# Moving two small tiles and shortening a constants vector in a two-layer encoder kernel

## The chip, the cores and the metric

One core of a Trainium2 chip runs the whole program in one launch. The metric is device time in microseconds (us). [...]

## The reference

Two layers over 256 tokens of width 1024, all in float32. Each layer normalises, projects once into three groups of heads and adds the output projection; then follows a channel mixer, dense in layer 0 and a mixture of eight experts (two for each token) in layer 1.

```
for l in range(2):
    h = rmsnorm(x, norm_mix[l]); proj = h @ w_in
    x = x + concat([rwkv7(proj), diff_attention(proj), pool(proj)]) @ w_out[l]
    h = rmsnorm(x, norm_ffn[l])
    if l == 0: x = x + (silu(h @ w_gate) * (h @ w_up)) @ w_down
    else:      x = x + sum_e combine[:, e] * swiglu(h, expert e)   # top 2 of 8 by h @ router
return rmsnorm(x, norm_out)
```

## The kernel before, in words

**Matmuls.** A product of two float32 matrices is split into high and low halves of type float32r (`mm3`, line 266 and after): high by high, high by low, low by high, three matmuls that add up in one PSUM bank. `wload` (line 186) brings a weight tile of 512 KB into a raw tile by a DMA on SP's queue (line 197), ScalarE casts it to the high half (line 200), VectorE or GpSimd subtracts to get the low half (line 208). In the dense layer's gate and up products the weight halves are the stationary operand and the layer's input `fT` (256 columns) is the moving one; in its down product, and in the experts, the weight halves move (512 columns). `plain` (line 179, DMA on line 183) loads weights that are used as float32, without the split, for the experts with few tokens.

**Order of the work.** The sequence of TensorE is written out by hand. SP's queue takes the weight loads in program order, and one load that waits holds up all behind it. VectorE, ScalarE and GpSimd (POOL) also run their own instructions in order.

**Memory.** A partition of SBUF is filled from below by pools in the order in which they are opened: constants (`const`, with `x`, `ident`, `vecs`, `dvecs`, ...), the ring of weight tiles (`ring`: 4 raw, 3 high, 3 low tiles of 4096 bytes), the mixers' pool (`mixc`), and above it the pool of the present stage (`mix0`, `ffn0`, `mix1`). Every tile takes a multiple of 32 bytes. In the kernel before, the constants end at byte 26880 and the ring at 67840, both multiples of 256, and `mixc` begins there. In `mixc` stand, in order of first use, `hT_h` and `hT_l` (8192 bytes each, the normalised input's halves, at 67840 and 76032), `Z`, `vfirst`, the tile with tag `G` (at 92416; it holds `u`, then the dense layer's input `fT`, then `xT`), `rst`, `consts` (109824 to 114752), then the small tiles `i4` (114752, 128 bytes), `rksel`, `dtmp` (64 bytes), `nlam`, `sin`, `cos` and a filler `mcpad`. The stage pools begin at 115200, also a multiple of 256. `x` and `ident` stand at 128 mod 256.

After layer 1's mixer the pool `mixc` is closed, and the pool of the experts takes its place from 67840 on: first `tri` (512 bytes), a few small tiles, the one-hot matrices, and then 4096-byte tiles for weights, `r0`, `r1`, ... A new tile waits for the last readers of the older tiles whose bytes it covers (`reuse_waits="tile"`), and for no others. `LOADS` gives the order in which weight loads take the tiles: `r17`, `r18`, `r19`, `r5`, two of the ring's own, `msilu`, and so on, 28 entries. `r18` covers bytes 114176 to 118272.

**The start of the experts.** `i4` is read for the last time by the matmuls that add up the router's logits at the end of `outproj` (line 225 by way of `mm`, tile `i`). The routing is then: `lg` on VectorE, the comparisons `cmp` (lines 1443 to 1446), `rank`, `sel`, a product with `tri` on TensorE, the one-hot `Pm`, the gather. On POOL stand in this order: the load of `router` (line 1004) and its product with the gains (line 1005), two low-half splits (line 208), `one` (line 1390), `tri` (line 1392), the low halves of `x` (line 1424), two more splits (line 208).

Of the kernel before, what the change touches and what calls it, by code (L numbers as in the profile page):

```python
# [7 lines left out]
F32 = mybir.dt.float32  # L8
# [97 lines left out]
class K:  # L106
# [172 lines left out]
    def setup_x(self, P):  # L279
        nc, A, cp, mc = self.nc, self.A, self.cp, self.mc  # L280
        x = self.x = cp.tile([128, 2, D], F32, name="x")
        self.ident = cp.tile([128, 128], F32, name="ident")
        nc.sync.dma_start(self.ident, A["consts"][:, C_ID:C_ID + 128])
        self.v = cp.tile([128, NROWS], F32, name="vecs")
        dv = self.dv = cp.tile([128, 64], F32, name="dvecs")
        nc.vector.memset(dv[:, 43:59], -0.5)
        nc.vector.memset(dv[:, 42:43], -math.log(2.0))
        xv = A["x"][0].rearrange("(a p) d -> p a d", p=128)

        rows = P.tile([NROWS, 128], F32, name="rows", tag="at", bufs=2)  # L290
        nc.sync.dma_start(rows, A["rows"])
        for a in range(2):
            nc.sync.dma_start(x[:, a], xv[:, a])
        pb = self.bank("pr")
        self.tr(pb[:, :NROWS], rows, self.ident[:NROWS, :NROWS])
        nc.vector.tensor_copy(self.v, pb[:, :NROWS])

    def setup(self, P):
        nc, A, cp, mc, v, dv = self.nc, self.A, self.cp, self.mc, self.v, self.dv

        self.Z = mc.tile([128, 3, 2, 2, 128], F32, name="Z")
        self.vfirst = mc.tile([128, 2, 256], F32, name="vfirst")
        mc.tile([128, 4096], F32, name="G0", tag="G")
        self.rst = mc.tile([128, 256], F32, name="rst")
        c = self.c = mc.tile([128, C_W], F32, name="consts")
        self.i4 = mc.tile([128, 32], F32, name="i4")
        self.rks, tmp = mc.tile([128, 4, 2], F32, name="rksel"), mc.tile([128, 16], F32, name="dtmp")
        self.nlam = mc.tile([128, 2], F32, name="nlam")
        self.sin, self.cos = (mc.tile([128, 2, 8], F32, name=n) for n in ("sin", "cos"))
        mc.tile([128, 16], F32, name="mcpad")  # L310
        nc.scalar.dma_start(c, A["consts"][:, :C_W])
        self.c2 = cp.tile([128, C_ALL - C_IOTA], F32, name="consts2")
        nc.scalar.dma_start(self.c2, A["consts"][:, C_IOTA:])

        sh = v[:, ROW_SHIFT:ROW_SHIFT + 32].rearrange("p (l i k) -> p l i k", l=2, i=2)
        self.tmp = tmp
        t2 = tmp.rearrange("p (l k) -> p l k", l=2)
        nc.vector.tensor_add(t2, sh[:, :, 0], sh[:, :, 1])
        nc.vector.tensor_scalar(dv[:, 0:16], tmp, -1.0, 1.0, op0=ALU.mult, op1=ALU.add)
        nc.vector.tensor_scalar(dv[:, 16:32], v[:, ROW_DEC:ROW_DEC + 16], 0.5, None, op0=ALU.mult)  # L320
        nc.vector.tensor_scalar(dv[:, 32:36], v[:, ROW_KA:ROW_KA + 4], -1.0, 2.0, op0=ALU.mult, op1=ALU.add)
        nc.vector.tensor_scalar(dv[:, 36:40], v[:, ROW_RK:ROW_RK + 4], 0.5, None, op0=ALU.mult)
        nc.vector.tensor_scalar(dv[:, 40:42], v[:, ROW_VB:ROW_VB + 2], 0.5, None, op0=ALU.mult)

        rks = self.rks
        for i in range(4):
            nc.vector.tensor_scalar(rks[:, i, :], c[:, C_BLK:C_BLK + 128:64], dv[:, 36 + i:37 + i], None, op0=ALU.mult)
        with self.later():
            nc.gpsimd.memset(self.Z, 0.0)
        nc.vector.memset(self.rst, 1.0)  # L330
        nc.vector.memset(self.rst.rearrange("p (c t) -> p c t", t=64)[:, :, 0:1], 0.0)
        nc.vector.tensor_reduce(self.i4, self.ident.rearrange("p (g t) -> p t g", t=32), axis=AX.X, op=ALU.add)
# [1521 lines left out]
    def build(self):  # L1854
        nc, tc, cp = self.nc, self.tc, self.cp
        mixers = ExitStack()
        mc = self.mc = mixers.enter_context(tc.tile_pool(name="mixc", bufs=1))
        for l in range(DEPTH):
            with tc.tile_pool(name=f"mix{l}", bufs=1, reuse_waits="tile") as P, self.psum(f"pm{l}", pq=2, at=2, pr=3, py=1):
                self.mixer(l, P)  # L1860
            if l == DEPTH - 1:
                mixers.close()
            if self.stop == f"mix{l}":
                mixers.close()
                return
            with tc.tile_pool(name=f"ffn{l}", bufs=1, reuse_waits="tile") as P:
                if l % 2 == 0:
                    with self.psum(f"pf{l}", pa=4, pr=4):
                        self.ffn(l, P)
                else:  # L1870
                    with self.psum(f"pf{l}", pg=4, py=2, px=2):
                        self.moe(l, P)
            if self.stop == f"ffn{l}":
                mixers.close()
                return
# [39 lines left out]
```

## Time and profile before

| what | us |
|---|---|
| median of 3 runs | 1556.11 (1555.88 to 1558.05) |
| the profiled execution, its own time | 1553.22 |
| its span, first to last instruction | 1551.4 |
| busy: TensorE, VectorE, ScalarE, GpSimd | 1463.6, 1003.6, 806.2, 178.4 |
| DMA traffic | 434.67 MB, mean 280 GB/s |

How to read it: the program goes through layer 0's mixer (to about 190 us), the dense layer (to 440), layer 1's mixer (to 628), and the experts (to the end). TensorE's busy share of 94% is an average over these; a stage may be held by the loads while TensorE looks busy, since a matmul's duration is longer than the distance to the next one's start. So the distance of starts is what tells TensorE's pace, and the windows' DMA share what the loads carry.

### The profile page before, as it was taken

The page shows a single profiled execution, that of the slowest core. Times are in us where ns is not written, and L with a number is a line of the kernel's source. Part 1 is how long each engine was busy: PE and PEld are TensorE (multiplying, and loading weights), DVE is VectorE, ACT ScalarE, POOL GpSimd, SP SyncE. Part 2 cuts the span into 40 slices and gives each one's busy share as a digit, 9 for nine tenths or more (in the row PEclk, how much of TensorE's full clock was granted, in tenths as well). Part 3 has the DMA queues.
Part 4 walks back from the last instruction along what each step waited for, and adds up shares of the span by engine and source line. Part 5 has one row for each costly group of instructions (what it writes and reads, how often), then busy time and mean ns, then how long its engine had stood idle before and what let it go on. Part 6 is the DMA issues. An engine that isn't in the chain of part 4 may idle for free.

```text
span 1551.4 us, 27151 instructions
## 1 busy us (share of the span) xinstructions
PE 1463.6 (94%) x10215; PEld 1111.4 (72%) x10215; DVE 1003.6 (65%) x1314; ACT 806.2 (52%) x1142; POOL 178.4 (11%) x161
## 2 busy tenths in 40 slices
PE   7799989999998999799999999999998999998996
PEld 6677889999986778688888743588634687435885
DVE  5865665556659746698899720699512898205896
ACT  4545454444445354587878510687302776205785
POOL 2532100000026423300001000001000010000001
PEclk9899999999998899899999999999999999999998
DMA  7322356666543230899999999999999999999991
GB/s 230 104 70 98 109 166 188 186 182 189 163 120 95 70 125 3 310 412 410 338 332 348 353 407 415 410 411 413 403 419 412 410 411 412 389 416 411 410 413 43
DMA packets 172457, 434.67 MB, mean 280 GB/s; under 512 B 14834, under 2 KB 18013, under 8 KB 172317
## 3 DMA queue, kind: packets, MB, share of 16 engines
q1 hardware_dynamic: 170924, 430.74, 74.4%
q8 instruction: 82, 1.34, 0.3%
q0 software_dynamic: 544, 1.12, 0.3%
q10 hardware_dynamic: 848, 0.99, 0.2%
q14 instruction: 59, 0.48, 0.1%
HBM read 431.75 MB, written 1.05 MB: 279 GB/s over the span
## 4 chain that ended last, share of the span: by engine, by line
PE 75%; DVE 9%; DMA 7%; ACT 3%; issue 3%; POOL 1%; ACTq 0%; SPq 0%; DVEq 0%; POOLq 0%
PE ps L225 72%; PE ps L229 3%; DMA r<-in_exp_up 2%; DMA raw<-in_exp_up 2%; DMA r<-in_exp_gate 2%; DVE wlo L208 2%; DVE wlox L208 1%; DMA posi<-in_positions 1%; ACT whi L200 1%; ACT whix L200 0%; DVE AR L655 0%; DMA x<-in_x 0%; DVE us L550 0%; DVE kd L659 0%; ACT Sf L761 0%
## 5 line engine op out<-in xcount | busy, mean ns | idle before, releaser
L208 DVE TENSOR_TENSOR wlo<-r,whi 128x1024 fp32r<-128x1024 f32 x192 | 234.6, 1248 | 42.3 <-ACT whi L200 41.1
L200 ACT CAST whi<-r 128x1024 fp32r<-128x1024 f32 x195 | 201.0, 1056 | 37.5 <-DMA r<-in_exp_gate 19.3
L208 DVE TENSOR_TENSOR wlox<-r,whix 128x1024 fp32r<-128x1024 f32 x120 | 147.1, 1246 | 65.3 <-ACT whix L200 64.2
L200 ACT CAST whi<-raw 128x1024 fp32r<-128x1024 f32 x119 | 124.7, 1052 | 97.4 <-PE ps L225 82.6
L208 DVE TENSOR_TENSOR wlo<-raw,whi 128x1024 fp32r<-128x1024 f32 x104 | 129.7, 1251 | 59.7 <-ACT whi L200 59.3
L200 ACT CAST whix<-r 128x1024 fp32r<-128x1024 f32 x120 | 124.5, 1056 | 36.9 <-DMA r<-in_exp_gate 25.1
L225 PE MATMUL ps<-whi,gf 128*128 128x512 f32 x400 | 137.2, 401 | 1.3 <-ACT whi L200 1.3
L225 PE MATMUL ps<-r,gs 128*64 128x512 f32 (+1 forms) x636 | 130.6, 541 | 2.6 <-DMA r<-in_exp_up 2.5
L225 PE MATMUL ps<-fT,whi 128*128 128x256 f32 x544 | 100.8, 287 | 4.7 <-DVE gu L1306 3.7
L1417 POOL TENSOR_TENSOR xp<-x,xp 128x512 fp32r<-128x512 f32 x12 | 24.3, 2026 | 631.6 <-ACT xp L1416 631.6
L225 PE MATMUL ps<-whix,gf 128*128 128x512 f32 x272 | 93.9, 400 | 2.5 <-ACT whix L200 2.5
L225 PEld LDWEIGHTS ps<-r,gs 128*64 128x64 f32 x636 | 42.8, 136 | 74.1 <-issue 58.3
L225 PEld LDWEIGHTS ps<-whi,gf 128*128 128x128 f32 x400 | 76.6, 191 | 21.9 <-ACT whi L200 2.9
L225 PEld LDWEIGHTS ps<-fT,whi 128*128 128x128 f32 x544 | 86.2, 194 | 6.0 <-issue 4.3
L1663 ACT COPY mah<-ps 128x512 f32<-128x512 f32 (+1 forms) x12 | 6.4, 532 | 143.9 <-PE ps L229 143.9
L225 PE MATMUL ps<-wlo,gf 128*128 128x512 f32 x200 | 79.6, 398 | 1.2 <-DVE wlo L208 1.1
L225 PE MATMUL ps<-fT,wlo 128*128 128x256 f32 x272 | 77.6, 285 | 0.0
L225 PE MATMUL ps<-whi,hT_h 128*128 128x512 f32 x160 | 69.6, 435 | 5.6 <-DVE up L1073 5.5
L208 DVE TENSOR_TENSOR wlox<-raw,whix 128x1024 fp32r<-128x1024 f32 x51 | 63.1, 1242 | 17.5 <-ACT whix L200 16.6
L225 PE MATMUL ps<-r,mah 128*64 128x512 f32 x276 | 64.8, 599 | 2.4 <-DMA r<-in_exp_down 2.0
L225 PE MATMUL ps<-whi,mah 128*128 128x512 f32 x170 | 66.5, 391 | 0.0
L225 PE MATMUL ps<-wlo,mah 128*128 128x512 f32 x170 | 66.4, 390 | 0.0
(468 smaller groups left out, 3400.3 us busy)
## 6 DMA issues: line engine op xcount, KB each, us to landing
r<-in_exp_down SPq DMA_DIRECT2D x178, 512.0 KB, 10.1
r<-in_exp_up SPq DMA_DIRECT2D x172, 512.0 KB, 10.0
r<-in_exp_gate SPq DMA_DIRECT2D x172, 512.0 KB, 10.0
raw<-in_exp_gate SPq DMA_DIRECT2D x43, 512.0 KB, 10.0
raw<-in_exp_up SPq DMA_DIRECT2D x43, 512.0 KB, 9.9
raw<-in_exp_down SPq DMA_DIRECT2D x37, 512.0 KB, 10.0
raw<-in_w_in_first SPq DMA_DIRECT2D x22, 512.0 KB, 4.3
raw<-in_w_in_rest SPq DMA_DIRECT2D x22, 512.0 KB, 3.6
```

The source lines that it names most:

```text
L200: w1 = nc.scalar.copy(hi[:, :a * b], raw[:, :a * b])
L208: w2 = (early or nc.vector).tensor_sub(lo[:, :a * b], raw[:, :a * b], hi[:, :a * b].bitcast(F32))
L225: self.nc.tensor.matmul(out, lhsT, rhs, start=start, stop=stop, skip_group_check=skip_group_check)
L229: self.nc.tensor.transpose(out, in_, ident)
L1417: nc.gpsimd.tensor_sub(xl, xs, xh.bitcast(F32))
L1663: nc.scalar.copy(at, b)
```

## The change

The constants vector `dvecs` becomes 56 columns instead of 64 (32 bytes shorter; its unused tail of -0.5 is shortened with it). `i4` and `dtmp` are allocated first in `mixc`, when that pool is opened, instead of in `setup`. No instruction but the one memset differs.

By the allocator's rules that makes these places: the ring, the stage pools, the experts' pool and the rest of `mixc`'s small tiles lie 32 bytes lower (weights at 224 mod 256); `mixc`'s large tiles, the dense layer's input among them, lie 160 bytes higher (160 mod 256).

```diff
-        dv = self.dv = cp.tile([128, 64], F32, name="dvecs")
-        nc.vector.memset(dv[:, 43:59], -0.5)
+        dv = self.dv = cp.tile([128, 56], F32, name="dvecs")
+        nc.vector.memset(dv[:, 43:56], -0.5)
...
-        self.i4 = mc.tile([128, 32], F32, name="i4")
-        self.rks, tmp = mc.tile([128, 4, 2], F32, name="rksel"), mc.tile([128, 16], F32, name="dtmp")
+        self.rks, tmp = mc.tile([128, 4, 2], F32, name="rksel"), self.dtmp
...
         mc = self.mc = mixers.enter_context(tc.tile_pool(name="mixc", bufs=1))
+
+        self.i4, self.dtmp = mc.tile([128, 32], F32, name="i4"), mc.tile([128, 16], F32, name="dtmp")
```

## Rows read from the trace of the kernel before

**Rows 1.** Windows: us, busy us of each engine (instructions), granted clock, DMA share, GB/s

```profile
590.00:628.00 38.00, 36.79 (x288) 30.09 (x287) 21.29 (x45) 16.75 (x30) 13.27 (x11) 1.00 0.02 2
645.00:753.00 108.00, 106.76 (x480) 88.33 (x481) 98.03 (x127) 83.17 (x90) 0.00 (x0) 0.98 1.04 411
753.00:892.00 139.00, 138.47 (x644) 111.92 (x644) 120.28 (x120) 101.35 (x127) 9.76 (x4) 1.00 0.93 335
892.00:1527.00 635.00, 618.67 (x2867) 385.16 (x2864) 360.13 (x358) 303.91 (x372) 14.56 (x8) 0.99 1.01 402
```

**Rows 2.** SP's queue, timeline 540 to 632: start us, duration us

```profile
562.24 0.71 SPq L197 DMA_DIRECT2D r<-in_exp_up  x1
628.14 0.37 SPq L197 DMA_DIRECT2D r<-in_exp_gate  x1
```

**Rows 3.** SP's waits, 560 to 640: us in total, times, longest

```profile
SPq L197 <- PE ps L225: 65.1, 1, 65.1
```

**Rows 4.** Tiles i4 (named i) and nlam: min/median/max ns, first and last start us

```profile
L225 PE MATMUL ps<-i,router x4: 256/256/277, 627.5 to 627.9; 128*128 128x8 f32 x4
L1208 DVE SCALAR_TENSOR_TENSOR lamr<-lamr,nlam,smx x8: 210/217/1320, 133.3 to 592.5; 128x2 f32<-128x2 f32 x8
```

**Rows 5.** SP's waits, 750 to 800

```profile
SPq L197 <- DVE wlo L208: 22.8, 14, 5.5
```

**Rows 6.** POOL, timeline 605 to 640: start us, duration us

```profile
608.21 1.01 POOL L1004 DMA_DIRECT2D router<-in_router  x1
611.46 0.67 POOL L1005 TENSOR_TENSOR router<-router,vecs 128x64 f32<-128x64 f32 x1 [2.24 <-DMA router<-in_router]
616.87 2.41 POOL L208 TENSOR_TENSOR wlo<-w4o,whi 128x1024 fp32r<-128x1024 f32 x1 [4.74 <-ACT whi L200]
...
624.36 0.62 POOL L1392 TENSOR_SCALAR tri<-consts,vecs 128x128 f32<-128x128 f32 x1
626.85 4.73 POOL L1424 TENSOR_TENSOR x<-x,x 128x1024 fp32r<-128x1024 f32 x2 [1.86 <-ACT x L1423]
```

**Rows 7.** Chain of waits in order of time: start us, length us

```profile
628.35 1.02 DVE cmp L1443
629.38 2.37 DVE cmp L1444
...
669.62 16.38 PE ps L225 x72
```

**Rows 8.** Page, part 6: loads, KB each, median us from issue to landing

```profile
r<-in_exp_down SPq DMA_DIRECT2D x178, 512.0 KB, 10.1
...
lnw<-in_lnx_w POOLq DMA_DIRECT2D x2, 128.0 KB, 6.1
```

**Rows 9.** TensorE, timeline 619.2 to 619.8

```profile
619.53 0.39 PE L225 MATMUL ps<-wlo,hT_h 128*128 128x512 f32 x1
```

**Rows 10.** TensorE, timeline 300 to 300.9; between the two rows lie eight matmuls

```profile
299.75 0.28 PE L225 MATMUL ps<-fT,wlo 128*128 128x256 f32 x1
...
300.83 0.28 PE L225 MATMUL ps<-fT,wlo 128*128 128x256 f32 x1
```

**Rows 11.** TensorE, timeline 653 to 655; between the two rows lie four matmuls

```profile
652.61 0.63 PE L225 MATMUL ps<-whi,gh 128*128 128x512 f32 x1
...
654.74 0.63 PE L225 MATMUL ps<-whi,gl 128*128 128x512 f32 x1
```

**Rows 12.** Window 194 to 440, instructions that read or write fT: PE, PEld, DVE, ACT

```profile
194.00:440.00 246.00, 165.47 (x1344) 163.93 (x1344) 3.19 (x12) 1.99 (x8) 0.99 0.57 172
```

**Rows 13.** TensorE by line, 194 to 440 and 645 to 892: count, busy us, mean ns

```profile
L229 PE MATMUL ps<-ident,x 128*128 128x128 f32 x10 | 1.4, 272 | 0.0
...
L229 PE MATMUL ps<-ident,msilu 128*128 128x128 f32 x52 | 7.8, 271 | 0.0
```

**Rows 14.** DMA queue 1 in 4 to 6.2 and 7 to 9: packets, MB, share of 16 engines

```profile
q1 hardware_dynamic: 295, 0.88, 102.0%
...
q1 hardware_dynamic: 230, 0.82, 101.2%
```

## The prediction

> **What bounds the kernel now.** I read the windows first, cut at the places where the DMA share changes, then SP's queue with its waits, then POOL's timeline and the chain of waits around the start of the experts, and last TensorE's starts. Three things are to be seen.
>
> Before the experts the loads stand still: from 590 to 628 us the DMA share is 0.02 [rows 1]. SP issued one expert load at 562.24 and the next at 628.14 [rows 2], held by a single wait on TensorE of 65.1 us [rows 3]. The load that waits is `r18`'s, and what it waits for is `i4`: the four matmuls that read it are the last before 628 [rows 4].
>
> From 645 to 892 us TensorE has no room (106.76 of 108 us, then 138.47 of 139), while the loads go from catching up (share 1.04) to waiting (0.93) [rows 1]. After 750 SP waits for low halves that have yet to free their raw tile, 22.8 us in 50 [rows 5]: by then the first round of tiles is full, and a load starts when a tile is free and not before.
>
> From 892 to 1527 the DMA engines are full, 1.01 of their span at 402 GB/s [rows 1]. That stretch is paid for in loads.
>
> **The change part by part.** The memset that is three columns shorter lies at the very start, while all engines wait for the first load; it is worth nothing, and without that cover a few ns. What is left is where tiles lie.
>
> *r18 no longer covers i4.* Shifted by 32 bytes it covers 114144 to 118240, where the tail of `consts`, `rksel`, `nlam`, `sin`, `cos` and the mixer's `us` stand. Of these `nlam` is read last, at 592.5 [rows 4]. So `r18`'s load goes at about 592.7 instead of 628.14, 35.4 us earlier, and what is queued behind it on SP follows as its tiles come free. A load of 512 KB takes 1.28 us at 411 GB/s [rows 1], so up to 27 of the first 28 could land before 628. What is it worth? The late loads are caught up by 753 in the kernel before, and until then TensorE is busy all the time [rows 1, 5]; a lead in loads is lost when all tiles are full, which is then the case some 60 us sooner. The work that ends the time stays TensorE until 892, and from there loads that begin as tiles come free, as before. I put it at nothing; what is late next is the routing, below. Bounds: no gain, and at most the 35.4 us by which the loads begin sooner, if the stretch after 892 really began with a debt of loads; since SP waits for tiles at 750 to 800, I take zero.
>
> *tri now covers i4.* `tri`, at the front of the experts' pool, lies on `i4`'s new place, so POOL's `tri` at 624.36 [rows 6] must wait for the matmuls that end at 628.1 [rows 4]: 3.8 us later. Queued behind it on POOL are the two low halves of `x` (4.73 us together) and two splits. Who waits for POOL here is VectorE: the first comparison takes 1.02 us and the second, of the same shape, 2.37 [rows 7], ending at 629.37 and 631.75, each just behind the end of a POOL instruction on `x` (626.85 plus 2.37 is 629.2, and 631.6) [rows 6]. With POOL moved by 1.9 us (`x` starts at 628.75 instead of 626.85), the first comparison can run behind `tri`, at 628.8, the second behind the first half of `x`, at 631.1: the routing ends within 0.3 us of before. If it comes in one POOL turn later, it costs 2.4 us. I take zero, since the order of who waits for whom is kept.
>
> *The router's load.* It leaves POOL at 608.21 and lands by 611.46 [rows 6], in a stretch with empty DMA engines. With the freed loads they are full then. The nearest row of a POOL load beside other traffic is 6.1 us, that of loads at full DMA 10.1 [rows 8]. At 6.1 it lands at 614.3, its product (0.67) is done at 615.0, and the split behind it starts at 616.87 all the same, because it waits for ScalarE [rows 6]. I take that, zero; the upper end is in the rivals.
>
> *Where operands lie.* For 256 columns the starts are (300.83 - 299.75)/9 = 0.120 us apart [rows 10], for 512 columns 16.38/72 = 0.2275 [rows 7]: 0.107 for the further 256, so 0.013 us a matmul comes on top of the columns. Every float32r operand of the kernel before starts at 0 mod 256, so no row shows another place. Of float32 there are transposes of `x` at 128 mod 256 and of `msilu` at 0, and they last 272 and 271 ns [rows 13]. From that row I take no effect; the ends are the whole 0.013 lost or once more added, as rivals.
>
> *Where loads land.* `x` is loaded to 128 mod 256, the first weights to 0. From 4 to 6.2 us (nearly all `x`) the DMA engines moved 0.88 MB in 102.0% of 16 x 2.2 us, 24.5 KB per engine and us; from 7 to 9 (weights) 0.82 MB in 101.2% of 16 x 2, 25.3 [rows 14]. The first window also holds 57 more packets under 2 KB, which move less in their time, so between nothing and 3%; I take nothing. [...]
>
> Sum: 0 + 0 + 0 + 0. The profiled execution's own 1553.22 would stay, which lies 2.9 under the median of the runs; the forecast goes by the median, **1556.1 us**.
>
> **The rivals.**
>
> *Faster, TensorE's 0.013 us shrinks.* For: it is not there at the lower clock, where 512 columns are (654.74 - 652.61)/5 = 0.426 apart [rows 11], just twice 0.213; so it looks like something beside the array, perhaps the two operands' reads meeting, and in the dense layer the change sets them apart by 64 bytes. In the experts both move alike, and after 892 TensorE isn't the bound. Against: it is the same for 256 and 512 columns, and the transposes show nothing. Price: 1344 matmuls in the dense layer [rows 12] x 0.0134 = 18.0 us if it goes, half of that 9.0; I take three quarters, 13.5: 1542.6. Layer 0's and 1's projections could add to it.
>
> *Slower, the router's weights come late.* Place: POOL's product with `router`, which stands ahead of the split that TensorE reads at 619.53 [rows 9]. At 10.1 us the load lands at 618.3, product and split end at 618.3 + 0.67 + 2.41 = 621.4, so TensorE waits 1.9 us; with a POOL turn of 2.4 lost in the routing, 4.3: 1560.4. It decides once the load takes over 8.0 us (landing after 616.2). For: full engines from 593 on. Against: the row of 6.1.
>
> *Slower, TensorE's extra part doubles*, since all operands now start off a multiple of 64 bytes: 18.0 us in the dense layer, 1574.1. The rows of 128 mod 256 say nothing on that.
>
> [...]
>
> *The change does nothing of what its places say*, the pools being rounded in another way: 1556.1, inside the forecast.
>
> **How the numbers follow.** No effect that can be told has 0.42: that is the forecast. The faster rival has 0.30. Slower has 0.28: the router 0.15, the doubled part 0.08, the loads 0.05. A measurement of this kernel can tell about 0.2%, 3.1 us, from no change. The range goes from 1540, which holds most of the faster rival, to 1572, which holds the router's case and the lower half of the doubled part; it leaves out the faster rival's end (about 0.06), the upper half (0.04) and the loads (0.05). The forecast's own range is 1553 to 1559.
>
> **What would show each step.** SP's queue should go on at about 592.7 and the DMA share of 590 to 628 rise to near 1; if it doesn't, the step on `r18` is wrong. POOL's `tri` should start at about 628.15, and `sel` end within 0.3 us of before. The DMA share after 753 should be as before; a full share and an earlier 892 would prove the lead worth something. Starts in the dense layer 0.120 apart say that places don't matter to TensorE; 0.107 or 0.133 prove a rival. [...] The forecast is wrong if the dense layer's length changes by over 3 us or if the first expert starts over 3 us from 645.

## The result and the profile after

The changed kernel takes 1568.68 us (median of 6 runs, 1566.51 to 1571.33), the kernel before 1557.07 beside it (6 runs, 1555.88 to 1559.49): 1.0074 times as long, 95% interval 1.0057 to 1.0091. It is 0.74% slower, where the forecast was 1556.1, no change that can be told, in a range from 1540 to 1572.

The profiled execution of after took 1571.33 us, with a span of 1569.5. The spans of the two profiled executions differ by 18.0 us and the medians by 11.6, because after's profile is the slowest of its six runs and before's, 1553.22 us, is faster than any of its six; the mixers of layer 0 hold that scatter (one kernel, profiled twice below as e1 and e11, reached its dense layer at 194.6 and at 201.8 us). It goes with TensorE's granted clock (a share of full speed; in the records of before and after every stretch has 1.0 or 0.5) from 0 to 190 us: 0.96 in before and 0.92 in after, 0.95 and 0.92 in those two. So the stages are compared from a mark of their own. The marks are first and last starts on TensorE: the dense layer's (`fT`), the first expert's (`gh`) and those of the experts with few tokens (`gs`). First before, then after.

```profile
L225 PE MATMUL ps<-fT,whi x544: 277/283/415, 194.8 to 418.4; 128*128 128x256 f32 x182
L225 PE MATMUL ps<-fT,wlo x272: 278/283/415, 195.2 to 418.5; 128*128 128x256 f32 x136
L225 PE MATMUL ps<-whi,gh x138: 388/389/632, 645.2 to 880.6; 128*128 128x512 f32 x138
L225 PE MATMUL ps<-r,gs x636: 379/592/644, 886.8 to 1394.3; 128*64 128x512 f32 x117, 128*64 128x256 f32 x42
```

```profile
L225 PE MATMUL ps<-fT,whi x544: 276/281/416, 199.9 to 419.6; 128*128 128x256 f32 x182
L225 PE MATMUL ps<-fT,wlo x272: 276/281/415, 200.3 to 419.7; 128*128 128x256 f32 x136
L225 PE MATMUL ps<-whi,gh x138: 388/389/628, 643.8 to 879.7; 128*128 128x512 f32 x138
L225 PE MATMUL ps<-r,gs x636: 379/592/643, 885.9 to 1410.9; 128*64 128x512 f32 x117, 128*64 128x256 f32 x42
```

| from | to | before, us | after, us | difference |
|---|---|---|---|---|
| start | first dense matmul | 194.8 | 199.9 | +5.1 (scatter) |
| first dense matmul | last | 223.7 | 219.8 | -3.9 |
| last dense matmul | first expert's first | 226.7 | 224.1 | -2.6 |
| first expert | first matmul of `gs` | 241.6 | 242.1 | +0.5 |
| first matmul of `gs` | end of the span | 664.6 | 683.6 | +19.0 |

Without the first line the sum is 13.0 us, near the 11.6 of the medians. Two stretches became shorter, and the last one, where loads are the limit (DMA share 1.03 in both), ate both and more. The windows of after answer to [rows 1]:

```profile
590.00:628.00 38.00, 37.04 (x277) 30.36 (x280) 21.70 (x48) 16.21 (x33) 12.94 (x10) 1.00 0.88 319
645.00:753.00 108.00, 106.90 (x485) 88.45 (x484) 97.12 (x126) 82.90 (x89) 0.47 (x1) 0.98 0.95 345
753.00:892.00 139.00, 138.32 (x640) 110.92 (x640) 121.19 (x121) 101.34 (x126) 8.29 (x4) 1.00 0.90 318
892.00:1527.00 635.00, 606.78 (x2784) 366.84 (x2781) 345.81 (x343) 292.40 (x357) 14.60 (x8) 0.99 1.03 398
```

The loads now run from 595 us on, and from 753 they wait for tiles as before (SP for low halves from 750 to 800: 26.0 us, 22.8 before). After 892 the engines for transfers are as full as ever, 1.03 of their span, and move less. The clearest view is the one of the transfers from 900 to 1500 us, before and after:

```profile
DMA packets 91740, 246.38 MB, mean 411 GB/s; under 512 B 7498, under 2 KB 7498, under 8 KB 91694
q1 hardware_dynamic: 91694, 245.82, 103.1%
```

```profile
DMA packets 88564, 239.07 MB, mean 398 GB/s; under 512 B 7284, under 2 KB 7284, under 8 KB 88521
q1 hardware_dynamic: 88521, 238.54, 103.0%
```

The same share of engine time carries 3.2% less. Counted packet by packet in the trace of that stretch: of the packets of 2048 bytes before, 99.8% took 84 ns or less, with a mean of 84.2; after, 28% did, 72% took 1 to 12 ns more, and the mean is 88.1. Those of 4096 bytes went from a mean of 160.7 to 163.7. The page's chain (part 4; before, then after) says what that does to the bound: the share of the transfers rose from 7% to 22%, that of TensorE fell from 75% to 58%.

```profile
PE 75%; DVE 9%; DMA 7%; ACT 3%; issue 3%; POOL 1%; ACTq 0%; SPq 0%; DVEq 0%; POOLq 0%
PE 58%; DMA 22%; DVE 10%; issue 4%; ACT 4%; POOL 1%; ACTq 0%; SPq 0%; DVEq 0%; POOLq 0%
```

The steps around 600 us. SP's queue, which answers to [rows 2], and its waits ([rows 3]):

```profile
564.03 0.73 SPq L197 DMA_DIRECT2D r<-in_exp_up  x1
594.77 0.37 SPq L197 DMA_DIRECT2D r<-in_exp_gate  x1
...
SPq L197 <- DVE lamr L1207: 29.9, 1, 29.9
```

`r18`'s load waits for `nlam`'s reader and no longer for `i4`'s. GpSimd ([rows 6]) and VectorE ([rows 7]):

```profile
610.22 1.01 POOL L1003 DMA_DIRECT2D router<-in_router  x1
616.64 1.05 POOL L1004 TENSOR_TENSOR router<-router,vecs 128x64 f32<-128x64 f32 x1 [5.41 <-DMA r<-in_exp_up]
618.92 2.41 POOL L208 TENSOR_TENSOR wlo<-w4o,whi 128x1024 fp32r<-128x1024 f32 x1 [1.23 <-ACT whi L200]
...
630.34 0.62 POOL L1391 TENSOR_SCALAR tri<-consts,vecs 128x128 f32<-128x128 f32 x1 [3.85 <-DMA r<-in_exp_up]
630.94 4.73 POOL L1423 TENSOR_TENSOR x<-x,x 128x1024 fp32r<-128x1024 f32 x2
```

```profile
630.48 0.38 DVE L1442 TENSOR_TENSOR cmp<-lg 128x128 f32<-128x128 f32 x1
630.77 0.28 DVE L1443 TENSOR_TENSOR cmp<-lg 128x128 f32<-128x128 f32 x1
631.09 2.37 DVE L1445 TENSOR_TENSOR cmp<-cmp,consts 128x128 f32<-128x128 f32 x1
...
633.95 1.75 DVE L1447 TENSOR_SCALAR sel<-rank 128x16 f32<-128x16 f32 x1
```

`tri` starts just behind the last matmul on `i4`, at 630.0. (The row names a load as what ended its wait, since that landed last by the profile; in e1, the experiment below with the same wait, the row names TensorE.) While `tri` waits, the subtractions on `x` behind it wait too, and two comparisons that took 1.02 and 2.37 us before take 0.38 and 0.28: both had begun when the first subtraction started, at 630.94. The row of e1:

```profile
628.26 0.62 POOL L1391 TENSOR_SCALAR tri<-consts,vecs 128x128 f32<-128x128 f32 x1 [3.86 <-PE ps L225]
```

From the last start on `i4` (627.9 before, 630.0 after) to the end of `sel` it was 8.4 us (636.3) and is now 5.7 (635.7).

### The profile page after: what moved, and what is told of

It is laid out like the page before. It is cut to its first block, busy times and chain, and to the rows that moved or that the text cites. A ratio compares the mean times of both kernels' runs of the same rounds, so it can differ in the third digit from the quotient of the medians.

```text
span 1569.5 us, 27154 instructions
## 1 busy us (share of the span) xinstructions
PE 1471.2 (94%) x10215; PEld 1107.3 (71%) x10215; DVE 1003.7 (64%) x1314; ACT 807.3 (51%) x1142; POOL 177.9 (11%) x161
## 4 chain that ended last, share of the span: by engine, by line
PE 58%; DMA 22%; DVE 10%; issue 4%; ACT 4%; POOL 1%; ACTq 0%; SPq 0%; DVEq 0%; POOLq 0%
PE ps L225 56%; DMA r<-in_exp_up 11%; DMA r<-in_exp_down 4%; DMA r<-in_exp_gate 3%; DVE wlo L208 3%; PE ps L229 2%; DVE wlox L208 1%; DMA raw<-in_exp_up 1%; ACT whi L200 1%; DMA raw<-in_exp_down 1%; DMA posi<-in_positions 1%; ACT whix L200 1%; DMA x<-in_x 0%; DVE us L549 0%; DMA raw<-in_w_in_first 0%
## 5 line engine op out<-in xcount | busy, mean ns | idle before, releaser
L1416 POOL TENSOR_TENSOR xp<-x,xp 128x512 fp32r<-128x512 f32 x12 | 22.9, 1907 | 640.3 <-ACT xp L1415 473.9
L208 DVE TENSOR_TENSOR wlox<-raw,whix 128x1024 fp32r<-128x1024 f32 x51 | 63.1, 1242 | 18.1 <-ACT whix L200 17.6
```

What stands on the lines that cost most here:

```text
L208: w2 = (early or nc.vector).tensor_sub(lo[:, :a * b], raw[:, :a * b], hi[:, :a * b].bitcast(F32))
L1416: nc.gpsimd.tensor_sub(xl, xs, xh.bitcast(F32))
```

## The experiments

Theory 1: the loads are slower because they land off a multiple of 256 bytes. Theory 2, its rival: they are slower because the loads set free at 595 us come in another order and meet later ones.

**The two parts of the change, taken apart.** The first run undoes the shorter vector and keeps the moved tiles; the second does the shorter vector alone. The next two shift the experts' pool alone, by 16 and 8 columns.

```diff
--- after
+++ e1
-dv = self.dv = cp.tile([128, 56], F32, name="dvecs")
-nc.vector.memset(dv[:, 43:56], -0.5)
+dv = self.dv = cp.tile([128, 64], F32, name="dvecs")
+nc.vector.memset(dv[:, 43:59], -0.5)
--- before
+++ e2
-dv = self.dv = cp.tile([128, 64], F32, name="dvecs")
-nc.vector.memset(dv[:, 43:59], -0.5)
+dv = self.dv = cp.tile([128, 56], F32, name="dvecs")
+nc.vector.memset(dv[:, 43:56], -0.5)
--- e1
+++ e3
+P.tile([128, 16], F32, name="pad0")
 tri = P.tile([128, 128], F32, name="tri")
```

> The changed kernel with the vector of constants at its old 64 columns: i4 and dtmp stay at the front of the mixers' pool, so the weight tiles lie at 0 mod 256 again, the dense layer's input at 192, and r18's load still goes early. Theory 1 (the place where loads land): after 892 us the loads run at 411 GB/s as before the change, packets of 2048 bytes take 84 ns and of 4096 bytes 159; time 1549 to 1556. Theory 2 (the loads set free at 595 us come to lie against later ones): the rate stays at 398 GB/s, time 1565 to 1571.

> The kernel before with the vector of constants 8 columns shorter and nothing else: everything from the ring up lies at 224 mod 256, r18's load still waits for the last reader of i4 until 628 us. Theory 1 (place): 398 GB/s after 892, mean packet 88 ns for 2048 bytes and 163 for 4096, time 1568 to 1574. Theory 2 (early loads): 411 GB/s, time 1553 to 1558.

> As the run with the vector at 64 columns, but with a tile of 64 bytes at the front of the experts' pool that nothing uses: the loads into that pool (81% of those after 892) land at 64 mod 256, those into the ring at 0. If loads want a multiple of 64 bytes: 411 GB/s and the time of the run with 64 columns within 3 us. If they want a multiple of 128 or 256: 400 GB/s, 12 to 18 us slower than that run. Theory 2 says nothing of a difference between the two.

> The same with 32 bytes instead of 64: the loads into the experts' pool land at 32 mod 256, those into the ring at 0. Theory 1: 400 GB/s after 892 whatever the multiple is (64, 128 or 256), 12 to 18 us slower than the run with 64 columns and no tile. Theory 2: no difference from that run.

All stages are measured as in the table above, the rate from 900 to 1500 us. The last four rows belong to experiments told further down. The time of before is that beside after; beside e1 to e4 it was 1556.05, beside e5 to e8 1557.40.

| run | loads land at | time, us | ratio to before | GB/s | dense layer | first expert to `gs` | `gs` to end |
|---|---|---|---|---|---|---|---|
| before | 0 | 1557.07 | | 411 | 223.7 | 241.6 | 664.6 |
| after | 224 | 1568.68 | 1.0057 to 1.0091 | 398 | 219.8 | 242.1 | 683.6 |
| e1, vector of 64 | 0 | 1548.45 | 0.9939 to 0.9976 | 411 | 220.3 | 242.2 | 664.7 |
| e2, vector of 56 alone | 224 | 1578.74 | 1.0098 to 1.0159 | 398 | 224.3 | 242.1 | 682.0 |
| e3, experts' pool + 64 | 64, ring 0 | 1564.53 | 1.0035 to 1.0072 | 404 | 220.5 | 245.3 | 675.0 |
| e4, experts' pool + 32 | 32, ring 0 | 1568.24 | 1.0049 to 1.0095 | 403 | 220.4 | 243.8 | 677.8 |
| e5, experts' pool + 128 | 128, ring 0 | 1567.52 | 1.0040 to 1.0092 | 404 | 220.7 | 245.1 | 675.2 |
| e6, experts' pool + 192 | 192, ring 0 | 1566.63 | 1.0038 to 1.0083 | 403 | 220.0 | 244.2 | 676.4 |
| e7, dense input at 128 | 0 | 1553.64 | 0.9965 to 0.9995 | 411 | 223.3 | 240.1 | 664.1 |
| e8, dense input at 224 | 0 | 1552.36 | 0.9958 to 0.9987 | 411 | 222.2 | 241.6 | 664.2 |

The transfers of e1, e2 and e3 from 900 to 1500 us:

```profile
DMA packets 92117, 246.64 MB, mean 411 GB/s; under 512 B 7510, under 2 KB 7510, under 8 KB 92073
```

```profile
DMA packets 87986, 238.83 MB, mean 398 GB/s; under 512 B 7271, under 2 KB 7271, under 8 KB 87942
```

```profile
DMA packets 89990, 242.35 MB, mean 404 GB/s; under 512 B 7382, under 2 KB 7382, under 8 KB 89947
```

The early loads are in e1 (DMA share 0.94 from 590 to 628 us) and not in e2 (0.02), the slow stretch is in e2 and not in e1: theory 2 falls, the place of the landing is the cause. And a multiple of 64 is not enough: e3 moves 404 GB/s, e1 411. The moved tiles are a gain: e1 is 0.43% faster than the kernel before. Misses: e2 took 4.7 us over its upper end. The interval of its ratio reaches down to 1571.3 us, inside the expectation; and its profile has 3.2 us more than before's up to the dense layer and 3.7 more from there to layer 1's last projection, at a lower granted clock (0.93 against 0.96 from 0 to 190 us, 0.90 against 0.94 from 449 to 583), as in the scatter above. That the shorter vector has no part in this isn't shown. e4 came 1.8 us over its upper end (19.8 us above e1), e1 0.5 under its lower one; e3 and e4 moved 404 and 403 GB/s where 400 was expected.

**Which multiple, and what made the routing shorter.** e5 and e6 are e3 with 32 and 48 columns in the pad. `tri` then lies clear of `i4`, while `r18` stays free.

> As the run with 64 columns, with 128 bytes at the front of the experts' pool: its loads land at 128 mod 256, and tri no longer lies on i4 (it need not wait for the matmuls that read it). Loads: if they want a multiple of 128, 411 GB/s and packets of 84 and 159 ns after 892; if they want a multiple of 256, 403 GB/s and the time from the first expert to the end 13 to 17 us longer than the 906.9 us of the run with 64 columns. Routing: if the 2.7 us that it gained come from tri's wait (which lets the first two comparisons slip in ahead of GpSimd's subtraction on x), sel ends 11.9 us after the second mixer's last projection as before the change; if they come from the early loads, 9.2 us as in the run with 64 columns.

> The same with 192 bytes: the experts' loads land at 192 mod 256, tri lies clear of i4. Whatever multiple over 64 is wanted, 403 GB/s after 892 and 13 to 17 us more from the first expert to the end than with 0; sel 11.9 us after the mixer's last projection if tri's wait was the gain.

128 and 192 cost what 32 and 64 cost (404 and 403 GB/s), so of the places tried only 0 mod 256 (411) is free. From the first expert to the end e5 took 920.2 us and e6 920.6 against 906.9, 13.3 and 13.7 more. And with `tri` not waiting, the routing is as long as before, though the loads were early. VectorE in e5:

```profile
629.02 1.01 DVE L1443 TENSOR_TENSOR cmp<-lg 128x128 f32<-128x128 f32 x1
629.96 2.45 DVE L1444 TENSOR_TENSOR cmp<-lg 128x128 f32<-128x128 f32 x1
632.44 2.33 DVE L1446 TENSOR_TENSOR cmp<-cmp,consts 128x128 f32<-128x128 f32 x1
```

Both ended `sel` 11.9 us after the mixer's last projection, e1 9.2. So the 2.7 us are `tri`'s wait.

**The dense layer's input.** e7 puts `dtmp` back behind the constants, e8 adds 32 bytes behind it at the front; the weights stay at 0.

```diff
--- e1
+++ e7
-self.rks, tmp = mc.tile([128, 4, 2], F32, name="rksel"), self.dtmp
+self.rks, tmp = mc.tile([128, 4, 2], F32, name="rksel"), mc.tile([128, 16], F32, name="dtmp")
...
-self.i4, self.dtmp = mc.tile([128, 32], F32, name="i4"), mc.tile([128, 16], F32, name="dtmp")
+self.i4 = mc.tile([128, 32], F32, name="i4")
--- e1
+++ e8
-mc.tile([128, 16], F32, name="mcpad")
+mc.tile([128, 8], F32, name="mcpad")
...
 self.i4, self.dtmp = mc.tile([128, 32], F32, name="i4"), mc.tile([128, 16], F32, name="dtmp")
+mc.tile([128, 8], F32, name="pad1")
```

> The run with 64 columns, with dtmp back behind the constants: weights at 0, the dense layer's input at 128 mod 256 (hT too). If any offset from the weights is enough: starts of 117 to 118 ns in the dense layer, its matmuls 220.5 us from first to last, total within 2 us of the run with 64 columns. If it is a question of 64 (odd or even multiples), 120 ns and 224 us as with equal places, total 3.5 us more.

> The run with 64 columns, with 32 more bytes behind dtmp: weights at 0, the dense layer's input at 224 mod 256, off a multiple of 64 alone. If any offset is enough: 220.5 us for the dense layer as at 192. If the input must start at a multiple of 64: over 222 us.

With the input at 192 from the weights (e1, e3 to e6, e10, e11; after with 160 against 224) the dense layer takes 219.2 to 220.7 us, at 0 (before; e2, where both lie at 224) 223.7 to 224.3, at 128 223.3, at 224 222.2. The granted clock doesn't make that difference: it is 0.99 over the layer in before, after and e7, and 0.98 in e1, e2 and e8. So it is the place of one operand against the other's that counts, not the place itself. In both runs the second reading came true, in e8 barely: 128 gains next to nothing and 224 a part, so not any offset will do. The starts of after at 300 us, which answer to [rows 10], show the same in small: (300.86 - 299.80)/9 = 0.118 us apart instead of 0.120. Taken over all starts from 260 to 400 us that lie under 0.2 us apart, the mean is 119.96 ns in before, 119.95 in e2, 119.96 in e7, 117.8 in after and e1 and 118.3 in e8. These 2.2 ns are 2.9 us in 1344 matmuls; the rest of the 3.9 isn't accounted for.

```profile
299.80 0.28 PE L225 MATMUL ps<-fT,wlo 128*128 128x256 f32 x1
...
300.86 0.28 PE L225 MATMUL ps<-fT,wlo 128*128 128x256 f32 x1
```

**Landings, or the engines' own reads.** In e9, here against e1, every tile that a load lands in lies at 0, and the ring's high and low halves, which no DMA writes, at 32.

```diff
 raw = self.raw_slot()
+if not hasattr(self, "pad2"):
+    self.pad2 = self.ring.tile([128, 8], F32, name="pad2")
...
-mc.tile([128, 16], F32, name="mcpad")
+mc.tile([128, 8], F32, name="mcpad")
...
+P.tile([128, 56], F32, name="pad0")
 tri = P.tile([128, 128], F32, name="tri")
```

> The run with 64 columns, with every tile that a load lands in kept at 0 mod 256, and the ring's high and low halves (written by ScalarE and VectorE, read by TensorE, by no DMA) at 32. tri lies clear of i4. Theory 1 (the landings of loads alone): 411 GB/s after 892 and 906 to 908 us from the first expert to the end, as with everything at 0. Rival (tiles off a multiple of 256 cost by the reads and writes of the engines, which then hold up the loads): under 408 GB/s and over 911 us.

```profile
DMA packets 91339, 245.93 MB, mean 410 GB/s; under 512 B 7490, under 2 KB 7490, under 8 KB 91293
```

The rate holds (410 GB/s, e1 411), so reads and writes of the engines off the multiple don't hold up the loads. The time does not hold: 1558.17 us (ratio 0.9976 to 1.0010), and 911.6 us from the first expert to the end. (Of the 8.0 us against e11, measured beside it, some 3 are the routing, where `tri` lies clear of `i4` as in e5.) Some 3 of the 4.7 us too many against e1 lie in the stretch where TensorE is the bound (245.5 us to the first matmul of `gs`, against 242.2, both at a granted clock of 0.99). The stretch of 72 matmuls of [rows 7], 16.38 us long in before and in e1, is 16.70 in e9, as its chain of waits shows:

```profile
668.07 16.70 PE ps L227 x72
```

The same stretch takes 16.63 to 16.71 us in e3, e4 and e5, where the ring's halves lie at 0 and the experts' input at 64, 32 and 128, 16.55 to 16.58 in e6 with 192, and 16.37 in after, where both lie at 224. So an offset of 192 between TensorE's operands helps in the dense layer (256 columns, input moving: 219.2 to 220.7 us against 223.7) and hurts a little in the experts (512 columns, weights moving: 16.55 to 16.58 against 16.38 for 72). Neither theory had that.

**GpSimd and the comparisons.** e10, here against e1, writes the routing's comparisons ahead of GpSimd's subtractions on `x` and puts a copy of `sel` before those; e11 is e1 again, beside it.

```diff
+        cmp = P.tile([128, 2, NE, 2 * NE], F32, name="cmp", tag="PT", bufs=2)
...
...
+        nc.vector.tensor_scalar(sel, rank, 2.0, None, op0=ALU.is_lt)
...
-            nc.gpsimd.tensor_sub(x0[1][a], self.x[:, a], x0[0][a].bitcast(F32))
+        nc.gpsimd.tensor_copy(P.tile([128, 2, NE], F32, name="turn"), sel)
+        for a in range(2):
+            nc.gpsimd.tensor_sub(x0[1][a], self.x[:, a], x0[0][a].bitcast(F32))
```

> The run with 64 columns, with the routing's comparisons written ahead of the split of x, and a copy of sel on GpSimd ahead of GpSimd's two subtractions on x, so that these wait until sel is done. If VectorE's operations of the routing take 1 to 2.4 us because GpSimd runs a subtraction beside them: all three comparisons take 0.3 to 0.4 us, sel ends at about 6.5 us after the second mixer's last projection instead of 9.2, and the first expert starts 1.5 to 2.5 us sooner (the subtractions end at 635 to 636 and hold it then), total 1546 to 1548. If they are slow for a cause of their own: no change from the run with 64 columns.

> The run with 64 columns once more, beside the one with the routing first, for their difference: 1547 to 1552 us, 0.3 to 0.6% under the kernel before.

GpSimd's timeline in e10, then VectorE's:

```profile
632.19 2.37 POOL L1433 TENSOR_TENSOR x<-x,x 128x1024 fp32r<-128x1024 f32 x1
635.44 0.20 POOL L1431 COPY turn<-sel 128x16 f32<-128x16 f32 x1 [0.88 <-DVE sel L1430]
635.61 2.37 POOL L1433 TENSOR_TENSOR x<-x,x 128x1024 fp32r<-128x1024 f32 x1
```

```profile
632.34 2.37 DVE L1428 TENSOR_TENSOR cmp<-cmp,consts 128x128 f32<-128x128 f32 x1
634.75 0.42 DVE L1429 TENSOR_REDUCE rank<-cmp 128x16 f32<-128x256 f32 x1
635.20 0.18 DVE L1430 TENSOR_SCALAR sel<-rank 128x16 f32<-128x16 f32 x1
```

Only half of the edit took effect: the first subtraction still ran ahead of the copy. It shows the wait all the better: the comparison that starts 0.15 us behind that subtraction takes 2.37 us and ends just behind it, and `sel`, which took 1.75 us beside the second subtraction, takes 0.18 with GpSimd idle. The first expert started 15.9 us after the mixer's last projection instead of 17.8 (e11). The total did not follow: 1551.32 us (0.9928 to 0.9963) against 1550.13 for e11 (0.9914 to 0.9961), and 1546 to 1548 expected. From the first expert to `gs` it took 244.3 us against 242.2, so the 1.9 us were lost again there. The granted clock of TensorE shows most of it: from 645 to 660 us it is 0.77 in e10 and 0.89 in e11, (0.89 - 0.77) x 15 = 1.8 us at full speed. In e10 TensorE had just stood idle for 2.18 us, waiting for VectorE's `rs`, and the matmuls behind that start 0.43 us apart until 656.7 us, the distance of [rows 11], where before's granted clock is 0.50 (652.6 to 655.4 us); in e11 the idle time was 1.10 us and such starts end at 657.2 but begin only at 653.8.

**Loads alone.** e12 leaves the whole computation out and moves 280 weight tiles, with nothing else running but, in the last two stretches, VectorE and ScalarE on other tiles.

```diff
...
+            for n in range(40):
+                t_ = tiles[n % 13]
...
+                    nc.sync.dma_start(t_, wd[e][:, n % 28])
...
+        phase(at0, 2048, 0)
+        phase(at224, 2048, 1)
+        phase(at128, 2048, 2)
+        phase(at0, 4096, 3)
+        phase(at224, 4096, 4)
+        phase(at0, 2048, 5, True)
+        phase(at224, 2048, 6, True)
```

> The computation is left out; the output is zeros. Seven stretches of 40 loads of 512 KB, one behind the other on SP's queue, each into 13 tiles in turn: rows of 2048 bytes at 0, at 224 and at 128 mod 256; rows of 4096 bytes at 0 and at 224; then rows of 2048 bytes at 0 and at 224 once more, with VectorE and ScalarE busy on other tiles that lie at 0. Theory 1a (a row off a multiple of 256 costs in itself when the engines for transfers are full): the stretches at 224 and 128 move 395 to 402 GB/s, those at 0 410 to 420, with idle engines as with busy ones; mean packet 88 against 84 ns. Theory 1b (it costs only where the loads meet the other engines' reads and writes of SBUF): the first five stretches are equal within 1%, and only the last one falls to 395 to 402.

Windows inside the seven stretches; the columns are VectorE, ScalarE, GpSimd, the granted clock, DMA share and GB/s:

```profile
10.00:50.00 40.00, 0.00 (x0) 0.00 (x0) 0.00 (x0) 1.00 1.05 408
60.00:100.00 40.00, 0.00 (x0) 0.00 (x0) 0.00 (x0) 1.00 1.05 387
110.00:150.00 40.00, 0.00 (x0) 0.00 (x0) 0.00 (x0) 1.00 1.05 387
170.00:205.00 35.00, 0.00 (x0) 0.00 (x0) 0.00 (x0) 1.00 1.03 420
225.00:255.00 30.00, 0.00 (x0) 0.00 (x0) 0.00 (x0) 1.00 1.03 409
265.00:310.00 45.00, 41.11 (x35) 40.61 (x39) 0.00 (x0) 1.00 1.05 408
320.00:355.00 35.00, 34.07 (x28) 33.99 (x33) 0.00 (x0) 1.00 1.05 387
```

Rows of 2048 bytes: 408 GB/s at 0, 387 at 224 and at 128, and the same again with the two engines busy. Rows of 4096 bytes: 420 at 0, 409 at 224. The mean packet is 84.0 ns at 0, 88.1 at 224 and 88.6 at 128 for the short rows, 159.0 and 163.1 at 0 and 224 for the long ones. So a row that lands at 224 instead of 0 costs 4.1 ns more in the mean, whether it has 2048 bytes or 4096, a short one at 128 4.6, and no other engine is needed for it. It is a mean: of the short rows at 224, 22% took 84 ns all the same. Theory 1a holds (its 395 to 402 for the short rows was too high: that is the rate of the kernel's mix of both).

## Why the prediction was wrong

*Where loads land: the step that failed.* The text bounded the effect by the window of `x`, "between nothing and 3%", and took nothing. It was 3.2%: 411 to 398 GB/s, and 19.0 us in the last stretch. The row could not carry the choice. It compared two windows of about 2 us and 230 to 295 packets; the same window of `x` gives 24.5 KB per engine and us in before and, in e1, where `x` lies in the same place, 0.85 MB in 105.4% of 16 x 2.2 us, 22.9. A row that scatters by 6.5% speaks neither for nor against 3%. The transfers were named as the bound after 892, so the upper end of the text's own range, 635 us x 3% = 19 us, was worth more than any other term, and no row set it at nothing. That the time came out inside 1540 to 1572 is luck: the range reached so high for the router's case and for half of the doubled extra part, neither of which came, and left the loads out.

*Of the slower cases that of the loads, 0.05, came nearest*, with too small a chance. It rested on an estimate that no run shows; what the runs show is a price for each row that lands off a multiple of 256. It measured 4.1 ns at 224, 4.9% of 84 and 2.6% of 159 (e12), and 32, 64, 128 and 192 cost alike (403 to 404 GB/s, 411 at 0). The last stretch is 2.9% longer (683.6 against 664.6 us). What the price is made of isn't shown.

*TensorE's starts.* "No effect" was wrong, and the faster rival right in its sign: the layer became 3.9 us shorter. Of the 0.0134 us that the text's estimate gave each of 1344 matmuls over its columns (0.0125 by [rows 7] and [rows 10], 0.120 - 0.426/4 = 0.0135 by [rows 10] and [rows 11]), 0.002 to 0.003 went, not three quarters (13.5 us). The reason it gave, that 64 bytes between the operands' places matter, is borne out (219.2 to 220.7 us at 192, in part at 224 with 222.2, and not at 0 or 128 with 223.7 and 223.3); what happens in the array's reads is not shown.

*`tri`.* The wait came, at 630.34, just behind `i4`'s readers. "The routing ends within 0.3 us of before" was wrong: it ended 2.7 us sooner. The working had the first comparison run behind `tri` and the second behind half of `x`. But VectorE was ready 0.14 us after `tri` began and its first two comparisons, 0.38 and 0.28 us long when undisturbed, had both begun before the subtraction on `x` did; only the third waited. In these runs it counts which of the two began first: the second comparison took 0.28 us where it began ahead of the subtraction (630.77 and 630.94), and 2.45 in e5, where it began at 629.96 amid the subtractions (627.50 to 632.26); the third of e10, 0.15 us behind one, took 2.37.

*`r18`.* Right. The load went at 594.77, which is the 592.7 of the text plus the 2.1 us by which this execution's mixer was later. The share from 590 to 628 rose to 0.88. The lead was worth nothing: with the loads early and landing at 0, e1 and e11 take 906.9 and 904.8 us from the first expert to the end, before 906.2.

*The router's load.* Right: 6.3 us from issue to landing where 6.1 was taken, and the split behind it still waited for ScalarE (1.23 us).

Put together with what the runs measured, the sum would be -3.9 (dense layer) - 3.5 (routing and what follows it, 20.7 to 17.3 us from the mixer's last projection to the first expert) + 19.0 (loads) = +11.6 us. The medians say +11.6, which by the ratio's interval is 8.9 to 14.2, so that the tenths agree is chance; left out are the mixers' scatter and 0.5 us in the experts' first stretch.

## What to carry to other kernels

Where loads are the bound, as here after 892 us, start every tile that a DMA lands in at a multiple of 256 bytes: 0 moved 411 GB/s, 224 398, and 32, 64, 128 and 192 in the experts' pool alone 403 to 404. A shift of 32 bytes far ahead in a pool cost 3 to 4 ns in the mean for each row of each load behind it (packets of 4096 bytes 160.7 to 163.7 ns, of 2048 84.2 to 88.1). A moved tile changes which older tiles it covers, so read off the waits that come and go; such a wait can be a gain when it keeps GpSimd's long instructions back while VectorE's short chain runs (here 8.4 to 5.7 us to the end of `sel`). The tiles' move without the shorter vector (e1, 1548.45 and again 1550.13 us) beats both kernels, by 0.4 to 0.6% against before.

## What was not expected of the hardware

- The price for a landing off 256 bytes shows in the stretch where the engines for transfers are full (share 1.03) and hardly in the dense layer. There (240 to 415 us, share 0.61 before and 0.64 after) 0.8% of the packets of 2048 bytes took 1 to 12 ns over 84 in after, 0.5% in before; in the full stretch it was 72%.
- With 81% of the loads off the multiple (e3 to e6) the last stretch is 11.4 us longer than in e1 on average, with all of them (after, e2) 18.1: that is 63%, not 81. The packets of 2048 bytes say the same, 46 to 49% of them over 84 ns against 71 to 72%. The part between is not explained.
- Two float32r operands at the same place mod 256 cost some 2 ns for 256 columns against the moving one 64 bytes below (119.96 and 117.8 ns from start to start). With 512 columns the same place is the fastest of those tried, and offsets of 32 to 192 cost 2 to 5 ns (16.55 to 16.71 against 16.38 us for 72).
